# A transformer block in float32: compression inputs and keys split at full width and copied between partitions by DMA, memory's sums of squares on ScalarE, softmax weights of two heads at a time

## The chip, the cores and the metric

One core of a Trainium2 chip runs the program. The metric is the time of one execution on the device in microseconds (us). The kernel before takes 458.88 us, the median of three runs (458.44 to 459.89).

The engines are TensorE (PE in the rows, its weight loads PEld), VectorE (DVE), ScalarE (ACT), GpSimd (POOL) and SyncE (SP). Each takes its instructions strictly in the order in which they stand in its queue, and each waits by semaphore for what an instruction needs. DMAs are issued from the queues of SyncE, ScalarE and GpSimd.

## The reference

One layer at width 1024 over 256 tokens: a sparse attention mixer ("NSA"), then cross attention to 256 memory tokens, then a gated feed-forward block with a three-tap convolution, with RMS norms between them and after the last. Only the first part and memory's norm are touched by the change:

```
h = rmsnorm(x)
q, kc, vc, ks, vs, kw, vw, gl = split(h @ w_in)          # q: 16 heads of 64; the others: 4 groups of 64
k_cmp = gelu(blocks(kc) @ ck_w1) @ ck_w2                 # blocks of 32 tokens, stride 16: 15 per group
v_cmp = gelu(blocks(vc) @ cv_w1) @ cv_w2
p_cmp = softmax(q . k_cmp);  p_sel = softmax(q . ks);  p_win = softmax(q . kw)     # per head, causal
o = g0 * p_cmp @ v_cmp + g1 * p_sel @ vs + g2 * p_win @ vw                         # g = sigmoid(gl)
x = x + o @ w_out
mem_n = rmsnorm(mem)
```

With 256 tokens all four selection blocks are always chosen and the window covers everything, so the selected and the window branch are both plain causal attention, each with its own keys and values.

## The kernel before, in words

**Float32 by halves.** Every product in full precision is made from rounded operands and their remainders: an operand `x` becomes `hi`, which ScalarE writes as a rounded copy, and `lo = x - hi`, which VectorE computes. `mm3` then issues three matmuls (hi.hi, lo.hi, hi.lo), on lines 187 to 189.

**Weights.** 512 KB half chunks (128 x 1024) come from HBM in one fixed order. `half` (line 127) loads each into `raw`, splits it with one ScalarE copy (line 120) and one VectorE subtraction (line 124), up to `AHEAD = 4` half chunks before TensorE uses it. There are `NBUF = 6` buffers of `hi` and of `lo`: half chunk number n takes the buffer of number n - 6 and so waits until TensorE has finished with that one. Numbered by chunk and half, the rows below have hi5 = keys of the selected branch (`w_ks`), hi6 and hi7 = the first weights of key compression (`w_ck`), hi8 and hi9 = of value compression (`w_cv`), hi10 = window keys (`w_kw`). So hi8_1 takes the buffer of hi5_1.

**Order of the work.** The queues of SyncE and GpSimd are filled in the order of the code. TensorE, VectorE and ScalarE are ordered at build time by a scheduler that runs a timeline of its own; the order is then fixed. In the first stage `between(first(), ...)` emits, a step at a time, the projections (`compress_in(0)`, `queries(0)`, `compress_in(1)`, `keys(0)`), then `hidden(0)` and `hidden(1)`, then `keys(1)` and `queries(1)`, and starts side jobs (`rms`, `gated`) at given steps; `later` hands it a job that runs on beside the stream.

**Compression inputs.** `compress_in(j)` (j = 0 for keys, 1 for values) makes `pc` in PSUM: 64 channels of two groups on partitions 0 to 63 and 64 to 127, tokens along the free axis. Line 462 multiplies it in place by the tokens' norm factor `row`. The hidden product needs another layout, `B[0]` (in the rows c200 for j = 0 and c210 for j = 1): even tokens on partitions 0 to 63, odd ones on 64 to 127. Four ScalarE copies of 64 partitions (two of them read one half of the partitions and write the other) make the hi part, four VectorE subtractions the lo part, all straight from PSUM. GpSimd copies the shifted second half of each block into `B[1]` (c201, c211; line 480) and puts the positional term `pe` into a spare column of `B[0]` (line 482).

**Hidden product.** `hidden(j)` takes `B` as the stationary operand, 32 matmuls into `pM` (line 531), two for every k tile. It uses eight half chunks in all for j = 0 and 1. A ScalarE copy `hsb` and two transposes into `pH` follow, then a short chain of GELU.

**Keys.** `keys(br)` multiplies `pk` by `row` into a spare tile, then ScalarE rounds it into `KH` and copies the other half of the partitions too (four copies of 64 partitions), and VectorE makes `KL` (two subtractions, line 509).

**Gates.** `gated` makes a small product `pg`, transposes it (`pgt`, just before the last four matmuls of `pk`), adds its two parts on VectorE, takes two tanh on ScalarE (line 597) and writes `gates` on VectorE (line 600).

**Attention.** 32 heads-and-tiles (`Head`) run as a software pipeline: scores, mask and row minimum on VectorE (line 826), exponent on ScalarE (line 832), then on VectorE a reciprocal, a product with the gate and two multiplications, one a branch (lines 837 to 840), then transposes on TensorE (line 846), a copy on ScalarE (line 850) and the value product (line 868). Between them `advance` hands TensorE a share of the projections for memory (`fill`) as filler.

**Memory's norm.** `mem_rms` takes half of each row's sum of squares on ScalarE and half on VectorE.

## Time and profile before

| | us |
|---|---|
| median of three runs | 458.88 |
| the profiled execution | 459.02 |
| its span in the trace | 457.1 |
| TensorE busy, of the span | 445.2 (97%) |
| VectorE, ScalarE, GpSimd busy | 324.2, 288.9, 42.7 |
| share of the chain that ended last on TensorE | 85% |

The profiled execution took 1.9 us more than its span, which is what lies around the span. The rows name lines of the kernel before, tiles without their buffer numbers, and say in brackets what ended an engine's wait. A TensorE row's duration includes the way through the array, so back to back matmuls overlap; how close they follow shows in their starts.

### The profile page before, as it was taken

The page shows a single profiled execution, that of the slowest core. Times are in us where ns is not written, and L with a number is a line of the kernel's source. Part 1 is how long each engine was busy: PE and PEld are TensorE (multiplying, and loading weights), DVE is VectorE, ACT ScalarE, POOL GpSimd, SP SyncE. Part 2 cuts the span into 40 slices and gives each one's busy share as a digit, 9 for nine tenths or more (in the row PEclk, how much of TensorE's full clock was granted, in tenths as well). Part 3 has the DMA queues.
Part 4 walks back from the last instruction along what each step waited for, and adds up shares of the span by engine and source line. Part 5 has one row for each costly group of instructions (what it writes and reads, how often), then busy time and mean ns, then how long its engine had stood idle before and what let it go on. Part 6 is the DMA issues. An engine that isn't in the chain of part 4 may idle for free.

```text
span 457.1 us, 8682 instructions
## 1 busy us (share of the span) xinstructions
PE 445.2 (97%) x3276; PEld 412.1 (90%) x3276; DVE 324.2 (71%) x694; ACT 288.9 (63%) x591; POOL 42.7 (9%) x82
## 2 busy tenths in 40 slices
PE   8999799999999999999999999999999999999994
PEld 5999799999998778999998899999999999888984
DVE  4788989798888895846643857878777777745413
ACT  6796689677887886865553757666666666535301
POOL 4332001221200000200000010000000000001003
PEclk9999899999999999999999999999999999999998
DMA  8997775543422005555334437755555555564302
GB/s 293 363 412 261 242 241 167 181 122 111 139 94 92 3 1 181 162 156 187 102 104 170 150 128 210 246 186 184 187 180 185 184 189 179 189 188 151 128 0 93
DMA packets 22077, 77.05 MB, mean 169 GB/s; under 512 B 2579, under 2 KB 3091, under 8 KB 22035
## 3 DMA queue, kind: packets, MB, share of 16 engines
q1 hardware_dynamic: 21312, 74.39, 48.7%
q10 hardware_dynamic: 720, 2.10, 1.4%
q8 instruction: 26, 0.43, 0.4%
q14 instruction: 19, 0.13, 0.1%
HBM read 75.43 MB, written 1.05 MB: 167 GB/s over the span
## 4 chain that ended last, share of the span: by engine, by line
PE 85%; DVE 6%; DMA 4%; ACT 2%; issue 2%; SPq 0%; POOLq 0%; DVEq 0%; ACTq 0%; POOL 0%
PE up L187 8%; PE up L189 8%; PE up L188 8%; PE pd L189 5%; PE pd L187 4%; PE pd L188 4%; PE O L868 2%; DVE lo L124 2%; PE pt L846 2%; DMA raw<-in_w_ks 2%; PE pcq L187 2%; PE pmk L189 2%; PE pmk L188 2%; PE pmk L187 2%; PE pmv L189 2%
## 5 line engine op out<-in xcount | busy, mean ns | idle before, releaser
L124 DVE TENSOR_TENSOR lo<-raw,hi 128x1024 fp32r<-128x1024 f32 x130 | 158.6, 1227 | 60.2 <-ACT hi L120 59.3
L120 ACT ACTIVATE hi<-raw 128x1024 fp32r<-128x1024 f32 x130 | 136.8, 1058 | 55.1 <-PE pd L189 17.7
L187 PE MATMUL up<-h_hi,hi 128*128 128x256 f32 x304 | 86.3, 284 | 0.0
L189 PE MATMUL up<-h_hi,lo 128*128 128x256 f32 x304 | 86.2, 284 | 0.0
L188 PE MATMUL up<-h_lo,hi 128*128 128x256 f32 x304 | 86.2, 284 | 0.0
L188 PEld LDWEIGHTS up<-h_lo,hi 128*128 128x128 f32 x304 | 58.4, 192 | 0.0
L189 PEld LDWEIGHTS up<-h_hi,lo 128*128 128x128 f32 x304 | 58.4, 192 | 0.0
L187 PEld LDWEIGHTS up<-h_hi,hi 128*128 128x128 f32 x304 | 58.4, 192 | 0.0
L189 PE MATMUL pd<-hi,aT_lo 128*128 128x512 f32 (+1 forms) x110 | 38.5, 350 | 0.0
L188 PE MATMUL pd<-lo,aT_hi 128*128 128x512 f32 (+1 forms) x110 | 38.5, 350 | 0.0
L187 PE MATMUL pd<-hi,aT_hi 128*128 128x512 f32 (+1 forms) x110 | 38.4, 349 | 0.0
L832 ACT ACTIVATE pp<-pp,nm 128x128 f32<-128x128 f32 (+1 forms) x64 | 28.4, 447 | 5.8 <-DVE nm L826 5.6
L826 DVE CUSTOM_DVE_ANT_0 pp<-s,tri,nrs 128x128 f32<-128x128 f32 (+1 forms) x64 | 24.1, 412 | 2.4 <-PE pt L846 2.0
L188 PEld LDWEIGHTS pd<-lo,aT_hi 128*128 128x128 f32 x110 | 20.7, 188 | 2.9
L189 PEld LDWEIGHTS pd<-hi,aT_lo 128*128 128x128 f32 x110 | 20.7, 188 | 2.9
L187 PEld LDWEIGHTS pd<-hi,aT_hi 128*128 128x128 f32 x110 | 20.7, 189 | 2.9
L1110 ACT ACTIVATE th<-c 128x256 f32<-128x256 f32 x22 | 9.1, 414 | 22.2 <-DVE c L1108 22.2
L850 ACT ACTIVATE pT<-pt 128x256 f32<-128x256 f32 (+1 forms) x32 | 15.3, 482 | 9.2 <-PE pt L846 8.9
L840 DVE TENSOR_SCALAR pp<-pp,den 128x128 f32<-128x128 f32 (+1 forms) x64 | 19.8, 349 | 0.6
L189 PE MATMUL pmv<-hi,memT_lo 128*128 128x256 f32 x64 | 18.6, 290 | 0.0
L188 PE MATMUL pmv<-lo,memT_hi 128*128 128x256 f32 x64 | 18.5, 289 | 0.0
L189 PE MATMUL pq<-hT_hi,lo 128*128 128x256 f32 x64 | 18.5, 289 | 0.0
(309 smaller groups left out, 1149.2 us busy)
## 6 DMA issues: line engine op xcount, KB each, us to landing
raw<-in_w_up SPq DMA_DIRECT2D x44, 512.0 KB, 4.6
raw<-in_w_dn SPq DMA_DIRECT2D x20, 512.0 KB, 3.8
raw<-in_w_q SPq DMA_DIRECT2D x8, 512.0 KB, 5.1
raw<-in_w_mk SPq DMA_DIRECT2D x8, 512.0 KB, 5.0
raw<-in_w_mv SPq DMA_DIRECT2D x8, 512.0 KB, 3.7
raw<-in_w_out SPq DMA_DIRECT2D x8, 512.0 KB, 3.8
raw<-in_ca_wq SPq DMA_DIRECT2D x8, 512.0 KB, 4.7
raw<-in_ca_wo SPq DMA_DIRECT2D x8, 512.0 KB, 4.2
```

The lines of the kernel that those rows point to most:

```text
L120: nc.scalar.activation(his[i][h], raws[i][h], AF.Copy)
L124: nc.vector.tensor_tensor(t, raws[i][h], f(his[i][h]), op=ALU.subtract)
L187: nc.tensor.matmul(ps, lh, rh, start=start, stop=False)
L188: nc.tensor.matmul(ps, lh, rl, start=False, stop=False)
L189: nc.tensor.matmul(ps, ll, rh, start=False, stop=stop)
L826: nc.vector.tensor_tensor_reduce(self.ppv[:, br], sv[:, br], tri[:, 1 - t:], nrs[:, t:t + 1], 3e38, ALU.add, ALU.min, self.nm[:, br:br + 1])
L832: nc.scalar.activation(self.ppv[:, br], self.ppv[:, br], AF.Exp, bias=self.nm[:, br:br + 1], scale=-1.0, accum_out=self.den[:, br:br + 1])
L840: nc.vector.tensor_scalar(self.ppv[:, br], self.ppv[:, br], den[:, br:br + 1], None, op0=ALU.mult)
L846: nc.tensor.transpose(self.pt[:, o:o + P], self.pp[:, o:o + P], ident)
L850: nc.scalar.activation(self.pT[:, :self.w], self.pt[:, :self.w], AF.Copy)
L868: nc.tensor.matmul(O[r:r + DK, m * P:(m + 1) * P], V[:, blk // 2, blk % 2, g, :], group[i].pT[:, blk * P:(blk + 1) * P], start=False, stop ...
L1110: nc.scalar.activation(th, c, AF.Tanh, scale=0.5)
```

## The change

Five things, in the words of the code. `CW = 6` is new.

1. `compress_in`: line 462's product goes to a spare piece of SBUF (`v`, in `xT`) with even and odd tokens apart, instead of back to PSUM. Four DMAs of 64 partitions, issued from GpSimd's queue, carry it into the layout of `B` (`vp`). After six steps one ScalarE copy and one VectorE subtraction at 128 partitions split it. GpSimd's copies become one for `B[1]` and one for `pe`. Columns are numbered by group, not by block (`NC` 60 becomes 64), and what reads them follows.
2. `keys`: the product is split at 128 partitions into a tile `T`, and six DMAs from GpSimd's queue carry T into `KH` (both halves of the partitions) and `KL`. `KH` and `KL` now hold the branches one after the other (`br`, then tile).
3. `mem_rms`: both sums of squares on ScalarE.
4. Heads in pairs: `weigh` once for two heads, with one product of two tensors in place of four multiplications by a column; `transposed` and `copied` in units of one full PSUM bank.
5. The pipeline's driver calls the pair's steps on every second turn.

```diff
@@ compress_in
-                B = [cp.tile([P, 8, 2, 64], F32R, name=f"c2{j}{i}") for i in range(2)]
+                B = [cp.tile([P, 8, 2, 2, 2, 16], F32R, name=f"c2{j}{i}") for i in range(2)]
+                rows = [z.rearrange("p jj x g m n -> p (jj x g m) n") for z in B]
...
                 def out(ps):
                     yield from wait("row")
-                    nc.vector.tensor_tensor(both, both, row.unsqueeze(1).to_broadcast([P, 2, S]), op=ALU.mult)
-                    split((B[1][:, :, 0, NC], B[1][:, :, 1, NC], cc[:, o + 8:o + 16]),
-                          (pe[:, 0, :, 0], pe[:, 1, :, 0], cc[:, o:o + 8]))
...
-                    for hi, lo, v_ in items:
-                        split_hi(hi, v_)
-                    yield
-                    for hi, lo, v_ in items:
-                        split_lo(lo, hi, v_)
-                    for x in range(2):
-                        nc.gpsimd.tensor_copy(B[1][:, :, x, 0:NC], f(B[0][:, :, x, G:16 * G]))
-                    for x in range(2):
-                        nc.gpsimd.tensor_copy(B[0][:, :, x, NC:NC + 1], f(pe[:, x]))
+                    v, vp = (xT[:, k:k + 2].rearrange("p k s -> p (k s)") for k in ((6, 2), (4, 6))[j])
...
+                    nc.vector.tensor_tensor(v.rearrange("p r m c -> p m c r"),
+                                            ps.rearrange("p (m c r) -> p m c r", m=2, r=2),
+                                            row.rearrange("p (c r) -> p c r", r=2).unsqueeze(1).to_broadcast(
+                                                [P, 2, 128, 2]), op=ALU.mult)
                     for gp in range(2):
                         for par in range(2):
...
+                            nc.gpsimd.dma_start(vp[par * 64:par * 64 + 64, gp].rearrange("p c jj -> p (c jj)"),
+                                              v[gp * 64:gp * 64 + 64, par].rearrange("p m c -> p (m c)"))
+                    split((B[1][:, :, 0, 0, 0, PEC], B[1][:, :, 1, 0, 0, PEC], cc[:, o + 8:o + 16]),
+                          (pe[:, 0, :, 0], pe[:, 1, :, 0], cc[:, o:o + 8]))
+                    yield from pause(CW)
+                    hi, lo = (B[0][:, :, x].rearrange("p jj g m n -> p g (m n) jj") for x in range(2))
+                    split_hi(hi, vp)
+                    yield
+                    split_lo(lo, hi, vp)
+                    nc.gpsimd.tensor_copy(rows[1][:, :, 0:PEC], f(rows[0][:, :, 1:16]))
+                    nc.gpsimd.tensor_copy(B[0][:, :, :, 0, 0, PEC].rearrange("p jj x -> p x jj"), f(pe[:, :, :, 0]))
                     done.add(f"c2{j}")
@@ keys
+                    T = xT[:, 4:8].rearrange("p (x m) s -> p x m s", x=2).bitcast(F32R)
+                    split_hi(T[:, 0], v)
+                    yield
+                    split_lo(T[:, 1], T[:, 0], v)
                     for gp in range(2):
...
-                        split_hi(hi, v_)
-                        items.append((hi, lo, copy, v_))
-                    yield
-                    for hi, lo, _, v_ in items:
-                        KE.tensor_tensor(lo, v_, f(hi), op=ALU.subtract)
-                    for _, _, hi, v_ in items:
-                        split_hi(hi, v_)
+                        for x, z, r in ((0, KH, own), (0, KH, oth), (1, KL, own)):
+                            nc.gpsimd.dma_start(
+                                f(z[r].rearrange("p (m gp) b h k -> p m gp b (h k)", gp=2)[:, :, gp, br]),
+                                f(T[own, x]))
@@ mem_rms
-                    sums = [sumsq(mem[:, :512], f"mem{t}a"), sumsq(mem[:, 512:], f"mem{t}b", dve=True)]
+                    sums = [sumsq(mem[:, :512], f"mem{t}a"), sumsq(mem[:, 512:], f"mem{t}b")]
@@ Head, Pair
                 def weigh(self):
-                    den = self.den
+                    den, w = self.den, (1 + self.t) * P
                     nc.vector.reciprocal(den, den)
-                    nc.vector.tensor_tensor(den, den, gates[:, self.g, self.t, self.i, 1:3], op=ALU.mult)
-                    for br in range(2):
-                        nc.vector.tensor_scalar(self.ppv[:, br], self.ppv[:, br], den[:, br:br + 1], None,
-                                                op0=ALU.mult)
+                    nc.vector.tensor_tensor(den, den, gates[:, self.g, self.t, 2 * self.m:2 * self.m + 2, 1:3], op=ALU.mult)
+                    pv_ = self.pp.rearrange("p j b k -> p (j b) k")[:, :, :w]
+                    nc.vector.tensor_tensor(pv_, pv_, den.rearrange("p j b -> p (j b)").unsqueeze(2).to_broadcast(
+                        [P, 4, w]), op=ALU.mult)
...
+                    def pair(f, lag):
+                        if (n - lag) % 2 and 0 < n - lag < len(heads):
+                            f(pairs[(n - lag) // 2])
```

**How the queues change.** ScalarE's queue before, from the split of the selected keys' first weights on; c200 is `B[0]` of the keys, c210 of the values.

```order
L120 ACTIVATE hi5_0_363<-raw5_0_361 128x1024 [waits DMAHW3_49,DVE_49]
L192 ACTIVATE c200_256<-pc0_260 64x2x16x8 [waits DVE_49]
L120 ACTIVATE hi5_1_381<-raw5_1_379 128x1024 [waits DMAHW4_49]
...
L192 ACTIVATE c210_449<-pc1_453 64x2x16x8 [waits DVE_49]
L120 ACTIVATE hi7_0_523<-raw7_0_521 128x1024
L585 ACTIVATE gsb_583<-pg_559 96x256 [waits PE_49]
...
L120 ACTIVATE hi8_0_635<-raw8_0_633 128x1024 [waits DMAHW6_49,PE_49]
L120 ACTIVATE hi8_1_652<-raw8_1_650 128x1024 [waits DMAHW7_49,PE_49]
```

The same queue after the change, at the place where c200 and c210 stand now.

```order
L121 ACTIVATE hi8_0_627<-raw8_0_625 128x1024 [waits DMAHW6_49,DVE_49,PE_49]
L597 ACTIVATE gt_597<-gt_597,hrs_248 128x48 [waits DVE_49,Pool_49]
...
L121 ACTIVATE hi8_1_643<-raw8_1_641 128x1024 [waits DMAHW7_49,PE_49]
L193 ACTIVATE c200_256<-xT_100 128x64x8 [waits DMASW2_49,DMASW3_49,DMASW1_49,DMASW0_49]
L217 ACTIVATE sq_mem1a_1118,ss_mem1a_1117<-mem1_1049 128x512 [waits DMAHW2_49]
...
L193 ACTIVATE c211_446<-cc_71 128x8 [waits Pool_49]
...
L121 ACTIVATE hi9_1_678<-raw9_1_676 128x1024 [waits DMAHW1_49,PE_49]
L193 ACTIVATE c210_445<-xT_100 128x64x8 [waits DMASW6_49,DMASW7_49,DMASW5_49,DMASW4_49]
L193 ACTIVATE xT_100<-xT_100 128x512 [waits DVE_49]
L121 ACTIVATE hi10_0_693<-raw10_0_691 128x1024 [waits DMAHW3_49,PE_49,Activation_49]
L121 ACTIVATE hi10_1_709<-raw10_1_707 128x1024 [waits DMAHW4_49,PE_49,Activation_49]
L538 ACTIVATE hsb0_701<-pM0_624 128x256 [waits PE_49]
```

The split of c200 stood ahead of hi5_1 and stands behind hi8_1 now; that of c210 stood ahead of hi7_0 and stands behind hi9_1, ahead of the copy `hsb0` of the first hidden product.

GpSimd's queue before, from the norm factor's diagonal on.

```order
L247 TENSOR_SCALAR dg_x_391<-ident_74,rs_x_101 128x128 [waits Pool_49]
L480 CAST c201_257<-c200_256 128x8x60 [waits Activation_49]
L480 CAST c201_257<-c200_256 128x8x60 [waits DVE_49]
L482 CAST c200_256<-pe0_258 128x8 [waits Pool_49] x2
L443 TENSOR_SCALAR nrs_247<-rs_x_101 128x2
L444 TENSOR_SCALAR hrs_248<-rs_x_101 128x2
L456 MEMSET c211_450 128x16x3
```

The same stretch after the change, up to the first DMA of the values.

```order
L248 TENSOR_SCALAR dg_x_391<-ident_74,rs_x_101 128x128 [waits Pool_49]
L474 DMA xT_100<-xT_100 64x256 [waits DMAHW5_49,DMAHW2_49,DVE_49]
L474 DMA xT_100<-xT_100 64x256 x3
L443 TENSOR_SCALAR nrs_247<-rs_x_101 128x2
L444 TENSOR_SCALAR hrs_248<-rs_x_101 128x2
L483 CAST c201_257<-c200_256 128x64x15 [waits DVE_49]
L484 CAST c200_256<-pe0_258 128x2x8 [waits Pool_49]
L460 MEMSET c211_446 128x64
L474 DMA xT_100<-xT_100 64x256 [waits DMASW0_49]
```

The four DMAs for the values stand behind the two copies of the keys' blocks, which wait for VectorE's part of c200.

VectorE's queue after the change, at c200.

```order
L593 COPY gt_597<-pgt_591 128x96 [waits PE_49]
L594 TENSOR_TENSOR gt_597<-pgt_591,gt_597 128x96 [waits DVE_49]
L125 TENSOR_TENSOR lo8_0_631<-raw8_0_625,hi8_0_627 128x1024 [waits DMAHW6_49,Activation_49]
...
L125 TENSOR_TENSOR lo8_1_647<-raw8_1_641,hi8_1_643 128x1024 [waits DMAHW7_49,PE_49,Activation_49]
L197 TENSOR_TENSOR c200_256<-xT_100,c200_256 128x64x8 [waits DMASW2_49,DMASW1_49,DMASW3_49,DMASW0_49,Activation_49]
L497 TENSOR_TENSOR xT_100<-pk0_516,xT_100 128x512 [waits DVE_49]
```

The subtraction for c200, which stood third behind the product by `row` before, stands behind lo8_1 now. On TensorE the first matmul of the hidden product follows the last of `pk` directly, before and after, and waits for ScalarE's, VectorE's and GpSimd's parts of c200; after the change all 32 matmuls of the second hidden product stand behind the two transposes `pH` of the first.

## Rows read from the trace of the kernel before

**Rows 1.** The page's engine shares and the granted clock in 40 slices.
```profile
PE 445.2 (97%) x3276; PEld 412.1 (90%) x3276; DVE 324.2 (71%) x694; ACT 288.9 (63%) x591; POOL 42.7 (9%) x82
PEclk9999899999999999999999999999999999999998
```

**Rows 2.** Busy time by stretches: us, engines' busy us (instructions), clock, DMA, GB/s.
```profile
40.00:50.00 10.00, 8.47 (x66) 7.72 (x65) 8.76 (x12) 7.89 (x13) 3.69 (x4) 1.00 0.67 214
50.00:60.00 10.00, 8.44 (x54) 7.79 (x53) 8.68 (x17) 8.29 (x15) 0.00 (x0) 0.83 0.78 252
60.00:70.00 10.00, 10.00 (x86) 10.00 (x85) 9.73 (x18) 8.54 (x13) 0.00 (x0) 1.00 0.68 221
...
160.00:170.00 10.00, 9.38 (x75) 7.40 (x74) 9.70 (x47) 9.25 (x32) 0.27 (x1) 1.00 0.01 2
```

**Rows 3.** The same view in short stretches of the hidden products.
```profile
48.00:49.00 1.00, 0.18 (x1) 0.00 (x0) 1.00 (x2) 0.97 (x2) 0.00 (x0) 1.00 0.88 324
...
54.00:57.00 3.00, 3.00 (x16) 3.00 (x15) 3.00 (x5) 1.70 (x2) 0.00 (x0) 0.50 0.75 220
```

**Rows 4.** TensorE in order of time: start, us, operation, wait before it.
```profile
42.65 0.38 PE L589 MATMUL pgt<-ident,gsb 96*128 96x96 f32 x2 [0.39 <-ACT gsb L585]
...
43.25 0.28 PE L189 MATMUL pk<-hT_hi,lo 128*128 128x256 f32 x1
43.82 0.36 PE L531 MATMUL pM<-hi,c 128*128 128x256 f32 x1 [0.29 <-DVE c L196]
...
49.03 0.38 PE L531 MATMUL pM<-lo,c 128*128 128x256 f32 x1 [0.85 <-DVE lo L124]
...
52.30 0.44 PE L542 MATMUL pH<-ident,hsb 128*128 128x128 f32 x2
53.53 0.39 PE L531 MATMUL pM<-lo,c 128*128 128x256 f32 x1 [0.80 <-DVE lo L124]
...
63.15 0.28 PE L189 MATMUL pq<-hT_hi,lo 128*128 128x256 f32 x1
```

**Rows 5.** ScalarE in order of time, 27 to 53 us.
```profile
27.52 2.59 ACT L192 ACTIVATE c<-pc 64x256 fp32r<-64x256 f32 x4
...
39.17 0.33 ACTq L894 DMA_DIRECT2D mem<-in_mem  x1
...
43.75 1.99 ACT L120 ACTIVATE hi<-raw 128x1024 fp32r<-128x1024 f32 x2
...
49.68 0.56 ACT L597 ACTIVATE gt<-gt,hrs 128x48 f32<-128x48 f32 x2
50.26 0.63 ACT L192 ACTIVATE KH<-xT 64x512 fp32r<-64x512 f32 x1
```

**Rows 6.** VectorE in order of time, 27 to 53 us.
```profile
30.14 2.56 DVE L196 TENSOR_TENSOR c<-pc,c 64x256 fp32r<-64x256 f32 x4 [1.27 <-ACT c L192]
...
46.83 0.26 DVE L593 COPY gt<-pgt 128x96 f32<-128x96 f32 x1
...
52.26 1.22 DVE L124 TENSOR_TENSOR lo<-raw,hi 128x1024 fp32r<-128x1024 f32 x1
```

**Rows 7.** GpSimd in order of time, 16 to 46 us.
```profile
30.17 0.59 POOL L480 CAST c<-c 128x480 fp32r<-128x480 f32 x1 [5.74 <-ACT c L192]
32.76 1.65 POOL L480 CAST c<-c 128x480 fp32r<-128x480 f32 x1 [2.00 <-DVE c L196]
34.35 0.33 POOL L482 CAST c<-pe 128x8 fp32r<-128x8 f32 x2
```

**Rows 8.** DMA issues: queue, count, KB each, median us from issue to landing.
```profile
mem<-in_mem ACTq DMA_DIRECT2D x2, 512.0 KB, 6.7
...
out<-y SPq DMA_DIRECT2D x1, 256.0 KB, 2.0
```

**Rows 9.** Groups of instructions: busy us, mean ns of one, idle before them.
```profile
L840 DVE TENSOR_SCALAR pp<-pp,den 128x128 f32<-128x128 f32 (+1 forms) x64 | 19.8, 349 | 0.6
...
L837 DVE RECIPROCAL den<-den 128x2 f32<-128x2 f32 x32 | 5.1, 158 | 4.2 <-ACT pp L832 4.0
```

More of the change, by code (lines that the diff above doesn't have):

```diff
@@ L425, in trunk_kernel @@
             row = xT[:, 0]
-            free = [xT[:, k:k + 2] for k in (2, 4)]
             nrs = at.tile([P, NT], F32, name="nrs")
@@ L814, in scores @@
                     self.s = bank("S", f"s{self.name}")[:, :self.w]
-                    nc.tensor.matmul(self.s, q, khv, start=True, stop=False)
-                    nc.tensor.matmul(self.s, q, klv, start=False, stop=True)
+                    nc.tensor.matmul(self.s, q, KH[:, g, :, :n], start=True, stop=False)
+                    nc.tensor.matmul(self.s, q, KL[:, g, :, :n], start=False, stop=True)
                 def biggest(self):
-                    t = self.t
-                    self.pp = aq.tile([P, 512], F32, tag="pp", name=f"pp{self.name}", bufs=3)
@@ L821, in biggest @@
[L821 to L823 removed]
+                    pair, t, j = self.pair, self.t, self.i % 2
+                    if j == 0:
+                        pair.pp = aq.tile([P, 2, 2, 256], F32, tag="pp", name=f"pp{self.name}", bufs=2)
+                        pair.nm = small.tile([P, 2, 2], F32, tag="nm", name=f"nm{self.name}")
+                        pair.den = small.tile([P, 2, 2], F32, tag="den", name=f"den{self.name}")
@@ L872, in summed @@
-                def summed(self):
-                    g, tq = self.g, slice(self.t * P, (self.t + 1) * P)
-                    if self.i == HPG - 1:
-                        split((oT[0][:, 2 * g:2 * g + 2, tq], oT[1][:, 2 * g:2 * g + 2, tq],
-                               Os[g, self.t][:, :256].rearrange("p (c s) -> p c s", c=2)))
+                    blocks = [(j, br, h) for j in range(2) for br in range(2) for h in range(1 + self.t)]
+                    self.at = {b: divmod(n, 4) for n, b in enumerate(blocks)}
@@ new lines, in transposed @@
+                    self.pt = [bank("PT", f"pt{self.g}{self.t}{self.m}{n}") for n in range(len(blocks) // 4)]
+                    for (j, br, h), (n, o) in self.at.items():
+                        nc.tensor.transpose(self.pt[n][:, o * P:(o + 1) * P], self.pp[:, j, br, h * P:(h + 1) * P], ident)
+                def copied(self):
+                    self.pT = []
+                    for n, pt in enumerate(self.pt):
+                        self.pT.append(aq.tile([P, 4, P], F32, tag="pT", name=f"pT{self.g}{self.t}{self.m}{n}", bufs=5))
+                        nc.scalar.activation(self.pT[n].rearrange("p o k -> p (o k)"), pt, AF.Copy)
@@ new lines, in block, with values @@
+                def block(self, j, br, h):
+                    n, o = self.at[j, br, h]
+                    return self.pT[n][:, o]
+            def values(pairs_):
+                g, t = pairs_[0].g, pairs_[0].t
+                O = Os[g, t] = bank("O", f"O{g}{t}")
+                for m in range(2):
+                    nc.tensor.matmul(O[:, m * P:(m + 1) * P], Vc[:, g, m, :], pcT[:, g, t, :],
+                                     start=m == 0, stop=False, skip_group_check=True)
+                blocks = [(br, h) for br in range(2) for h in range(1 + t)]
+                for pair in pairs_[::-1]:
+                    for br, h in blocks:
+                        for j in (1, 0):
+                            nc.tensor.matmul(O[j * DK:(j + 1) * DK, pair.m * P:(pair.m + 1) * P], V[:, h, br, g, :],
+                                             pair.block(j, br, h), start=False, stop=(br, h) == blocks[-1],
+                                             skip_group_check=True)
@@ L928, in trunk_kernel @@
             UNITS = [(0, 0), (0, 1), (1, 0), (1, 1), (2, 0), (3, 0), (2, 1), (3, 1)]
-            heads = [Head(g, t, i) for g, t in UNITS for i in range(HPG)]
-            for n, h in enumerate(heads):
-                h.n = n
+            pairs = [Pair(g, t, m) for g, t in UNITS for m in range(2)]
+            heads = [h for pair in pairs for h in pair.heads]
             with tc.manual_schedule(engines=M2):
```

131 lines of the change are left out of this document (56 added, 75 removed).

## The prediction

> **What bounds the kernel now.** I read the page first: TensorE is busy for 97% of the span and its clock is full but for two slices [rows 1]. Busy time by tens of microseconds then tells where it is not: 1.5 us of 40 to 50 and 1.6 us of 50 to 60 are idle, the second of these at a mean clock of 0.83, while 60 to 70 is full with 86 matmuls, 0.116 us each; in 160 to 170 it lacks 0.6 us, with VectorE and ScalarE at 9.7 and 9.3 [rows 2]. So nearly everything is TensorE's own work, which the change leaves as it is (the same matmuls in another order). What it can win or lose lies in those two places.
>
> The first is the two hidden products. TensorE in order of time shows `pM` held up by weights that VectorE or ScalarE has not split: 0.85 us at 49.03 and 0.80 at 53.53, and only 0.29 us at its start, 43.82 [rows 4]. In short stretches TensorE does next to nothing in 48 to 49, and 54 to 57 runs at 0.50, the lower level of 1.2 GHz, with 16 matmuls in 3 us where the full level fits 26 [rows 3]. From `pM`'s start to the end of `pk` (63.15) 19.3 us pass; 64 matmuls of `pM`, 48 of `pk` and the small ones are 13.6 us at 0.116. So 5.7 us are lost there.
>
> **The change, part by part.** *Work taken off.* Eight copies of `c` at 0.65 us on ScalarE become two, eight subtractions at 0.64 on VectorE two [rows 5, 6]; the keys' copies of 0.63 go from eight to two; a sum of squares per memory tile moves to ScalarE. VectorE loses about 6 us of 27 to 60, ScalarE about as much. By busy time alone the 5.7 us would be there to win. But the engines take their queues in order, and the order has changed.
>
> *c200, first half.* ScalarE's part of c200 now stands behind hi8_1, and hi8_1 takes the buffer of hi5_1, which `pk` reads to its last matmul. I follow that. In the trace that matmul starts at 43.25; the transposes `pgt` ahead of it had waited 0.39 us for a ScalarE that was busy with c210, and that goes, so it starts at 42.85 and is through at 43.1, `pgt` at 42.6 [rows 4]. Ahead of hi8_1 stand the two tanh, which need `pgt`, then two small operations on VectorE, 0.26 us each [rows 6]: VectorE done at 43.2, tanh (0.56) at 43.8, hi8_1 (half of 1.99) at 44.8 [rows 5]. Then c200 on ScalarE to 45.7, while VectorE does lo8_1 (1.22) to 46.1 and then its part of c200 to 47.0 [rows 6].
>
> The price of these two full-width splits isn't in the trace. A copy of 512 elements in runs costs 0.63, one of 256 in the scattered layout 0.65 [rows 5]; so 0.63 if the scatter comes free now that the source is SBUF, 1.3 if it costs per element as before. VectorE's rows say 0.64 to 1.28 in the same way [rows 6]. I take 0.85 for each, nearer to the run of 512 since source and sink are both SBUF there.
>
> A rule bears on that choice. The Trainium skill (SBUF — State Buffer, section Door 1, on cachelines) says that an access which crosses to another 16-byte line pays, so that float32 may be strided only a little for free; each element of the new split is still written 512 bytes from the one before. By the rule it is 1.3 and the end comes 1 us later than in my sum; by the row of runs it is 0.63 and 0.5 us sooner.
>
> *c200, second half.* GpSimd must now wait for VectorE's part, copy 960 elements (two copies of 480 at 0.59 with no VectorE beside, so 1.2) and write `pe` (0.2 of 0.33) [rows 7]. Before, the first product's own copies were done at 34.7, nine microseconds early. Now they end at 48.4, and the first matmul of `pM` starts at 48.5 instead of 43.82: TensorE stands still for 5.4 us from 43.1 on.
>
> *c210.* The four DMAs for the values stand on GpSimd's queue behind those copies, so they cannot go out before 48.5 either, though their data has been ready since about 38. What one issue costs on GpSimd no row shows. ScalarE's queue issues one in 0.33 [rows 5]; a GpSimd instruction takes 0.2 to 1.65 [rows 7]. I take 0.7, twice ScalarE's, and keep 0.33 and 1.65 for the range: issued at 51.4. Landing took 2.0 us where the DMA engines were quiet and 6.7 where they were full [rows 8]; by then TensorE has stood still and loads wait for buffers, so 2.0: landed at 53.4. ScalarE, in order: c210 0.85, T 0.63, hi10_0 and hi10_1 2.0, and only then `hsb`, some 0.4; `pH` 0.44 [rows 4, 5]. So `pH` is through at 57.8. VectorE's and GpSimd's way to c210 (0.85 and 1.4 behind 54.3, and perhaps the waits of rival B) ends at about the same time. The first `pM` ends at 52.2 and the second starts at 57.8: another 5.6 us of standing still.
>
> *The sum in this place.* Second `pM` 3.7 us to 61.5, `pk` 5.6, transposes and the small key product 0.6: 67.7, against 63.3 for the same work before. That is 4.4 us lost, at full clock. The 5.7 us lost before include a stretch of 3 us at 0.50 that followed about 2.5 us of idling in 48 to 54 [rows 3]; with holes twice as long I expect the lower level again, and count the same 1.7 us where matmuls run: 6.1 us. If the level falls in the holes and is back when work is, it costs nothing; if it falls twice where matmuls run, 3.4.
>
> *c0's DMAs, the keys' DMAs, memory's sums.* The keys' four DMAs go out at 27, into full DMA engines; even at 6.7 us and more they have landed by 37, eight microseconds before ScalarE asks. The twelve DMAs into `KH` and `KL` are needed at the first scores, at 88 and later now; nothing on the way is late unless an issue costs over 1.5 us. Memory's squares lie in ScalarE's wait for c210. I count these at nothing; what hides them is the hole.
>
> *Heads in pairs.* The multiplications by a column, 19.8 us in 64, become 8 products of 512 elements (0.7, as a split of 512 costs) and 8 of 1024 (1.22), 15.4 us; reciprocals and gate products, 5.1 us and as much again, are halved [rows 6, 9]. VectorE has 9.5 us less over 85 to 170. TensorE is full for most of that with filler, so it counts only where filler has run out, in 150 to 170: 0.6 us are idle in 160 to 170, and the slice ahead of it is much the same, so some 1.3 [rows 2]. The order of pairs makes the steps coarser. I take 0.9 gained, of 0 to 1.3.
>
> Sum against the profiled execution: 459.0 + 6.1 - 0.9 = 464.2; its time is 0.1 above the median, so 464.
>
> **The rivals.** *A: the hole closes (faster).* If c200 and c210 were split long before `pk` ends, the work taken off would count in full: `pM` would start at 43.2 and run with `pk` to 57.1, 6 us sooner, and with the pairs the time would be 452. For it: VectorE full in 40 to 60 and the waits for lo [rows 2, 4]. Against it: the queue orders, in which only a wait for `pk`'s last buffer stands ahead of c200. It decides from the point where hi8_1 doesn't wait for hi5_1's last reader, or where the built order isn't the one that runs. 8%.
>
> *B: GpSimd's issues are dear.* A copy by GpSimd that takes 0.59 alone took 1.65 beside a VectorE split, 32.76 to 34.41, the length of that split and its own [rows 7]. If each of c210's four issues waits like that, they cost 1.65 each, 3.8 us more, and with some more for the keys' twelve the time is 468 to 469. Against it: few VectorE operations run in the hole. 22%.
>
> The Trainium skill (SBUF — State Buffer, section Who interferes with whom) says that GpSimd writes a DMA's descriptors through a port pair that VectorE's two-port operations lock, and that a two-tensor operation takes only the reading half of it; by that rule the splits don't hold the issues up, and B loses. No run here shows it yet.
>
> *C: the second hole is short.* With 0.33 an issue, 0.63 a split and no lower clock, the second `pM` starts at 55.5 and the end comes 2.1 later than before, less 1.3 from the pairs: 459.8, hardly to be told from no change. For it: the cheap ends are all from rows. Against: all three must come together. 10%.
>
> **How the numbers follow.** The forecast has 60%, with a range of its own of 461.5 to 467 (0.33 to 1 us an issue, clock loss 0 to 3.4). A measurement here tells 0.3%, 1.4 us, from no change. B lies above, C at the lower edge. A range of 460 to 469 leaves out A, the lower part of C and the worst of B, with everything dear (471). Faster by more than 0.3% is A: 0.08. Within it is most of C and a little of the forecast: 0.10. Slower: 0.82.
>
> **What would show it.** In the profile after: the first `pM` waits some 5 us with GpSimd's `pe` copy as its releaser, starting at 47.5 to 49.5; hi8_1 starts behind the tanh at about 43.8, c200 right behind it though its DMAs landed before 40; c210 waits on ScalarE for a DMA issued behind the copies; `pH` follows at 55 to 60; the granted clock falls in 45 to 65. In 150 to 170 TensorE's waits shrink by about a microsecond. I am wrong if c200 is split before 43, if TensorE starts `pM` before 46, or if the second hole is under 2 us; and wrong in size if an issue on GpSimd takes over 1 us or the level stays full.

## The result and the profile after

The kernel after took 466.7 us (median of 4 runs, 466.1 to 467.3) where the kernel before, on the same chip, took 459.0: a ratio of 1.016 (95% interval 1.0145 to 1.0179), 7.7 us slower. The prediction was 464.0 in a range of 460 to 469. The profiled spans are 457.1 and 465.0 us. Two profiled executions of the runs below, e1's (2464 us) and e9's (499 us), ran slow from end to end and are left out of the times.

The engine shares and the granted clock, after, against [rows 1]:

```profile
PE 445.1 (96%) x3276; PEld 413.3 (89%) x3276; DVE 314.6 (68%) x602; ACT 282.0 (61%) x575; POOL 49.6 (11%) x99
PEclk9999799989999999999999999999999999999998
```

VectorE has 9.6 us less to do, ScalarE 6.9, GpSimd 6.9 more; TensorE has the same. Less work made a longer kernel.

TensorE in order of time, after (start, us, operation, wait before it and its releaser), against [rows 4]:

```profile
42.72 0.28 PE L190 MATMUL pk<-hT_hi,lo 128*128 128x256 f32 x1
...
48.28 0.58 PE L531 MATMUL pM<-hi,c 128*128 128x256 f32 x1 [5.28 <-POOL c L484]
...
56.60 0.44 PE L542 MATMUL pH<-ident,hsb 128*128 128x128 f32 x2 [2.77 <-ACT hsb L538]
56.86 0.38 PE L531 MATMUL pM<-hi,c 128*128 128x256 f32 x1
...
91.05 0.46 PE L756 MATMUL psc<-ident,sT 64*128 64x64 f32 x4 [1.26 <-ACT sT L745]
```

The holes that the prediction named are there: 5.28 us ahead of the first `pM`, released by GpSimd's copy of `pe`, and 2.77 ahead of `pH`, behind which the second `pM` stands. A third place, at 91 us, is new. ScalarE in order of time, after:

```profile
43.65 1.04 ACT L121 ACTIVATE hi<-raw 128x1024 fp32r<-128x1024 f32 x1
44.60 1.09 ACT L193 ACTIVATE c<-xT 128x512 fp32r<-128x512 f32 x1
...
51.86 1.06 ACT L121 ACTIVATE hi<-raw 128x1024 fp32r<-128x1024 f32 x1 [0.63 <-PE pM L531]
52.83 1.14 ACT L193 ACTIVATE c<-xT 128x512 fp32r<-128x512 f32 x1
53.76 0.64 ACT L193 ACTIVATE xT<-xT 128x512 fp32r<-128x512 f32 x1
54.29 1.99 ACT L121 ACTIVATE hi<-raw 128x1024 fp32r<-128x1024 f32 x2
56.18 0.37 ACT L538 ACTIVATE hsb<-pM 128x256 f32<-128x256 f32 x1
...
85.04 3.31 ACT L193 ACTIVATE memT_hi<-MV,cc 128x256 fp32r<-128x256 f32 x8 [3.32 <-DMA KL<-xT]
```

Three queue orders are read here. c200 starts straight behind hi8_1, though its DMAs went out at 28; c210 straight behind hi9_1, with no wait for a DMA; and `hsb`, a copy of 0.37 us for which TensorE stands still, comes 3.4 us behind c210's start, behind three splits. GpSimd in order of time, after, against [rows 7]:

```profile
28.04 2.32 POOL L474 DMA_DIRECT2D xT<-xT  x4 [3.54 <-DVE xT L468]
...
46.97 0.98 POOL L483 CAST c<-c 128x960 fp32r<-128x960 f32 x1 [16.17 <-DVE c L197]
48.01 0.21 POOL L484 CAST c<-pe 128x16 fp32r<-128x16 f32 x1
...
48.25 2.10 POOL L474 DMA_DIRECT2D xT<-xT  x4
...
56.26 0.55 POOL L484 CAST c<-pe 128x16 fp32r<-128x16 f32 x1
```

GpSimd stood 16 us behind a wait with c210's four DMAs queued after it. The last row is its part of c210, which ends at 56.81: the second `pM`, at 56.86, could not have begun sooner had `hsb` come earlier. Short stretches, after (us; busy us and instructions of TensorE, its weight loads, VectorE, ScalarE, GpSimd; clock; DMA share; GB/s), against [rows 2, 3]:

```profile
48.00:51.00 3.00, 2.72 (x12) 2.72 (x13) 0.17 (x1) 1.04 (x2) 2.34 (x6) 0.50 0.77 244
...
57.00:60.00 3.00, 3.00 (x27) 3.00 (x27) 2.79 (x5) 0.10 (x1) 3.00 (x6) 1.00 0.69 197
...
92.00:96.00 4.00, 3.88 (x19) 3.82 (x20) 3.93 (x10) 3.11 (x8) 0.00 (x0) 0.58 0.74 224
```

Behind the first hole TensorE ran 12 matmuls in 3 us at the lower level, where 27 fit at the full one; behind the second the level stayed full; behind the third it fell again (0.58).

To see where time is lost and not won back, I added up the matmul columns of TensorE's timeline in each kernel (both have the same) and read how much later the other kernel reaches the same sum, at marks of the kernel before. "After" is 4.5 us behind at 60, 4.9 at 84.5, 8.0 at 96, and 7.5 at 441. The marks are good to some half a microsecond, since a column costs more in a short matmul (60 columns took 0.11 us, 256 took 0.12) and the two kernels have theirs in another order. So in this profile the loss has two parts: 4.9 in the hidden products, 3.1 near 91. The runs below that take one part away put the sizes otherwise: 6.9 for the compression inputs alone, 1.5 for the stall near 91.

The third place, in the chain of waits of after (start, us, what):

```profile
76.33 8.39 DMA KL<-xT
...
85.85 2.50 ACT memT_hi L193 x6
...
90.59 0.68 DVE QS L617
```

`T`, the source of the window keys' DMAs, lies in `xT`, and the memory's split `memT_hi` is written to the same place. It may not be written until the last DMA has read `T`; that one went out at 76.33 and was 8.39 us under way. In the kernel before this split starts at 72.00 with no wait.

### The profile page after: what moved, and what is told of

It reads as the page before. It is cut to its first block, busy times and chain, and to the rows that moved or that the text cites. A ratio compares the mean times of both kernels' runs of the same rounds, so it can differ in the third digit from the quotient of the medians.

```text
span 465.0 us, 8593 instructions
## 1 busy us (share of the span) xinstructions
PE 445.1 (96%) x3276; PEld 413.3 (89%) x3276; DVE 314.6 (68%) x602; ACT 282.0 (61%) x575; POOL 49.6 (11%) x99
## 4 chain that ended last, share of the span: by engine, by line
PE 86%; ACT 4%; DMA 3%; DVE 3%; issue 2%; POOL 1%; SPq 0%; POOLq 0%; DVEq 0%; ACTq 0%
PE up L190 8%; PE up L189 8%; PE up L188 8%; PE pd L188 4%; PE pd L189 4%; PE pd L190 4%; PE O L883 2%; PE pt L859 2%; PE pv L403 2%; DMA KL<-xT 2%; PE pmk L188 2%; PE pmk L189 2%; PE pmk L190 2%; PE pcq L188 2%; PE pcq L189 2%
## 5 line engine op out<-in xcount | busy, mean ns | idle before, releaser
L1164 POOL TENSOR_TENSOR xw<-x_sb,wfin 128x512 f32<-128x512 f32 (+1 forms) x2 | 3.9, 1952 | 155.7 <-DVE x_sb L1147 155.7
L189 PE MATMUL pmk<-memT_lo,hi 128*128 128x256 f32 x64 | 19.0, 297 | 0.0
L188 PE MATMUL pmk<-memT_hi,hi 128*128 128x256 f32 x64 | 18.8, 294 | 0.2 <-DVE QS L617 0.2
L190 PE MATMUL pmk<-memT_hi,lo 128*128 128x256 f32 x64 | 18.8, 294 | 0.0
```

Of the source, the lines that this page charges most:

```text
L188: nc.tensor.matmul(ps, lh, rh, start=start, stop=False)
L189: nc.tensor.matmul(ps, lh, rl, start=False, stop=False)
L190: nc.tensor.matmul(ps, ll, rh, start=False, stop=stop)
L1164: nc.gpsimd.tensor_tensor(xw[:, cs], x_sb[:, 1, cs], wfin[:, cs], op=ALU.mult)
```

## The experiments

The theory: the loss comes from where instructions stand in three queues, and from whose buffer `T` is; not from their durations, nor from the pairs of heads. The rivals: that the new operations (full-width splits, GpSimd's copies and issues) are dear by themselves, and that another part of the change carries part of the loss. Ratios are to the kernel before, with 95% intervals. Places are better evidence than the end of a single profile, since some profiles lose 1.0 to 1.6 us at 25 us (last section).

**The parts of the change.** e2 is the kernel before with the heads in pairs (and their layout of `KH` and `KL`) alone. Its edit is the diff's part at Head and Pair.

> The kernel before with the heads in pairs alone (and the new order of branches inside KH and KL that the pairs read). Theory M: the pairs are worth the 0.5 us by which the distance between the two kernels shrinks from 100 to 170 us: 458.5, no stall at 85 to 95. Rival R2 (the coarser steps cost the stall at 89 us): 461 to 462. A third reading, that the pairs' 9.5 us of VectorE are worth more where nothing else is late: 457 or less.

Measured: 459.05, ratio 0.9992 (0.998 to 1.0004). The pairs win nothing that ten runs can tell. e9 is the kernel before with the new compression inputs alone:

```
+  nc.gpsimd.dma_start(vp[...], v[...])     # four for each hidden product
   ...
+  yield from pause(CW)
   ...
+  split_hi(hi, vp); yield; split_lo(lo, hi, vp)
+  nc.gpsimd.tensor_copy(rows[1][:, :, 0:PEC], f(rows[0][:, :, 1:16]))
```

> The kernel before with the new compression inputs alone; keys, memory's sums and heads as before. Theory M (the holes in the hidden products are the inputs' work, the stall at 89 us that of the keys' DMAs): the first pM at 48 us, the second at 56 to 57, some 5 us lost there, and no stall at 89, since memory's split waits for no DMA: 464 to 464.5. Rival (the inputs carry the whole 7.7, and the keys' DMAs nothing, as the difference to the kernel with the old inputs says): 466 to 467. Rival (the parts need each other): under 461.

Measured: 466.1 (465.25 to 466.62, four runs), ratio 1.0151 (1.0126 to 1.0176). The inputs alone cost 6.9 us of the 7.7, and `memT_hi` waits for no DMA there. TensorE in order of time shows the same hole and releaser:

```profile
55.22 0.58 PE L534 MATMUL pM<-hi,c 128*128 128x256 f32 x1 [5.23 <-POOL c L485]
```

e3 is the reverse, the kernel after with the inputs as before:

```
-  split_hi(hi, vp); yield; split_lo(lo, hi, vp)
   ...
+  for hi, lo, v_ in items: split_hi(hi, v_)     # four of 64x256
+  yield
+  for hi, lo, v_ in items: split_lo(lo, hi, v_)
```

> The kernel after with the compression inputs as before (four copies and four subtractions out of PSUM, no DMA); keys by DMA, memory's sums and pairs stay. Theory M: the hidden products start at 43 to 44 us again and the 5.2 us lost there come back; the wait of memT for KL's DMAs stays: 461 to 462. Rival R1 (DMAs from GpSimd's queue as such are the cost, those of the keys as much as those of the inputs): 463.5 to 465, with the twelve that are left still disturbing. Rival R3 (the keys' or the sums' part opens the holes in the hidden products): no better than 466.

Measured: 459.24, ratio 1.0008 (0.9996 to 1.0021). All the rest of the change together costs nothing. By the columns it is 1.7 us ahead of the kernel before at 60 us, and 1.1 behind at 96: what is left of the change, the keys at full width among it, gains in the hidden products and gives it back later, where `memT_hi` starts at 81.31 instead of 72.00, though it waits for no DMA there; e7 below asks whether that is the cause.

**The third place.** e1 gives `T` of the second keys the buffer of c200, which is free by then:

```
+  if br:
+      T = cp.tile([P, 2, 2, S], F32R, tag="c200", name="T1")
```

> Edit: the second branch's split T goes to the buffer of c200, which is no longer read, instead of xT, whose place memory's split memT takes next. The DMAs into KH and KL stay. Theory M (the loss at 89 us is ScalarE's memT split waiting until the last DMA of KL has read T): ScalarE writes memT at about 73 instead of 85, TensorE's idling at 89 to 91 and the half clock behind it go, 3.1 us less: 463.6. Rival R1 (the DMAs into KH and KL are late in themselves, and the first scores wait for them): 466 to 467, with the wait moved from memT to the scores. Rival R2 (the pairs make the start of attention late): no change, 466.7.

Measured: 465.15 (464.4 to 465.7, three runs), ratio 1.0125 (1.0108 to 1.0142). About 1.5 us less than after; the expectation was 3.1. e11 is the same kernel once more, for its profile.

> The same kernel as in e1, for a profile: there the profiled execution ran at a sixth of TensorE's speed and shows nothing, while the timed ones gave 465.4 against 466.7 of the kernel after. Theory M: the wait of memory's split at 85 us is gone, and of the 3.1 us lost between 85 and 98 in the kernel after 1.3 are won; the rest is still lost at another place between 60 and 100. Rival: the wait stays, now for a later user of that place.

Measured: 465.59. `memT_hi` of e11, by tile (lines, first and last start), has lost its wait, and so has the clock's fall in 92 to 96:

```profile
L193 ACT ACTIVATE memT_hi<-MV,cc x8: 491/492/510, 73.7 to 77.4; 128x256 fp32r<-128x256 f32 x8
```
```profile
92.00:96.00 4.00, 4.00 (x31) 3.57 (x31) 3.89 (x11) 1.78 (x6) 0.00 (x0) 1.00 0.71 253
```

By the columns it goes from 6.0 behind at 84.5 to 6.3 at 96, where after goes from 4.9 to 8.0, so the stall's cause is shown. But this execution was 1.3 us late at 37 already; why the timed runs won 1.5 and not 3 the runs don't settle. e7 has the inputs as before and e1's buffer.

> The kernel with the old compression inputs (e3, 459.2), and besides the second branch's T in c200's buffer, so that memory's split doesn't wait for the DMAs that read T. In e3 this stretch (60 to 75 us) lost 2.8 us against the kernel before, and ahead of it the keys split at full width had won 1.5. Theory M: the loss goes, the gain stays: 456.5 to 457.5, faster than both kernels. Rival (the DMAs into KH and KL themselves, or the readers of KH, hold the attention up): 458.5 to 459.5. Rival (a later user of c200's place waits for them instead): 458 to 459, with the wait at the first heads' weights.

Measured: 458.9 (10 runs), ratio 1.0005 (0.9991 to 1.0018). `memT_hi` starts at 66.24 instead of 81.31, and that wins nothing that 10 runs can tell: its profiled execution, 1.2 us ahead by the columns at 441, is also the fastest of the ten. So the late `memT_hi` is not shown to be what e3 gives back; that stays open.

**The hidden products.** e4 moves c200's splits ahead of hi7_0 and lo7_0, and c210's ahead of hi9_0 and lo9_0:

```
+  early, AFTER = {}, {(7, 0): 0, (9, 0): 1}
   ...
+  with behind("hi", i, h):          # issued after the split of c2j0
       nc.scalar.activation(his[i][h], raws[i][h], AF.Copy)
   ...
+  with behind("lo", i, h):
       nc.vector.tensor_tensor(t, raws[i][h], f(his[i][h]), op=ALU.subtract)
```

> The kernel after, with issue order alone changed: on ScalarE and VectorE the split of c200 stands ahead of hi7_0 and lo7_0 and of the gates' copy, that of c210 ahead of hi9_0 and lo9_0, and the product for the keys behind lo8_0. Same instructions, same DMAs. Theory M (the place of c200's split behind pk's last buffer is the cause): first pM at 43 to 43.5 us instead of 48.3, the second, bound by the DMAs of c210 issued behind GpSimd's copies at 39 to 41, at about 50.5 instead of 57; the loss at 89 us stays: 460 to 462. Rival R1 (DMA traffic and the late loads of the weights are the cause, not the order): pM starts early but stalls for weights, 465 or more.

Measured: 469.12 (466.04 to 471.49), ratio 1.0223 (1.0163 to 1.0283). The first hole went, but the wait ahead of the second `pM` grew to 6.45 us. TensorE, GpSimd and ScalarE of e4, in order of time:

```profile
54.06 0.58 PE L540 MATMUL pM<-hi,c 128*128 128x256 f32 x1 [6.45 <-POOL c L492]
...
66.50 0.44 PE L551 MATMUL pH<-ident,hsb 128*128 128x128 f32 x2 [2.75 <-ACT hsb L547]
```
```profile
40.20 1.93 POOL L491 CAST c<-c 128x960 fp32r<-128x960 f32 x1 [8.77 <-DVE c L205]
...
43.29 2.11 POOL L482 DMA_DIRECT2D xT<-xT  x4
```
```profile
50.17 1.07 ACT L201 ACTIVATE c<-xT 128x512 fp32r<-128x512 f32 x1 [3.33 <-DMA xT<-xT]
...
65.12 1.06 ACT L126 ACTIVATE hi<-raw 128x1024 fp32r<-128x1024 f32 x1 [3.37 <-DMA raw<-in_w_q]
```

GpSimd's copies were twice as long beside VectorE's splits, c210's DMAs went out behind them at 43.29, and ScalarE waited for their landing. Here the step "c210 waits on ScalarE for a DMA issued behind the copies", which after itself does not show, decides over the second hole. It does not explain the time: by the columns (table below) e4 loses 1.7 us from 37 to 60, where after loses 4.4, and then 4.7 from 60 to 84.5, where after loses next to nothing. There the second `pH` waits 2.75 us for a `hsb` that stands on ScalarE behind a weight split, which waits 3.37 us for its load, and the clock behind it is 0.59 (68 to 72). e6 is after with those four DMAs ahead of GpSimd's copies, and nothing else; e5 is e4 with it:

```
+  done.add(f"in{j}")           # the DMAs of hidden product j are out
   ...
+  if j == 0:
+      yield from wait("in1")
   nc.gpsimd.tensor_copy(rows[1][:, :, 0:PEC], f(rows[0][:, :, 1:16]))
```

> The kernel after with the values' four DMAs ahead of GpSimd's copies and nothing else. Theory M: the first product isn't touched (c200's split is still behind hi8_1): 48.3 us. In the kernel after ScalarE came to c210 at 52.8 and didn't wait for its DMA, so the second hole is set by the queues of ScalarE and VectorE: no more than 1 us is won, 465.5 to 467. Rival (the prediction's step: the second hole is the DMAs issued behind the copies): second pM 2 to 3 us earlier, 463.5 to 464.5.

Measured: 468.32, ratio 1.0211 (1.0193 to 1.0228), 1.6 us more than after. TensorE of e6:

```profile
49.39 0.58 PE L534 MATMUL pM<-hi,c 128*128 128x256 f32 x1 [5.22 <-POOL c L487]
...
75.46 0.40 PE L663 MATMUL pvc<-w2v,gv 128*15 128x64 f32 x4 [0.80 <-POOL gv L656]
```

ScalarE's order keeps the first hole; ahead of `pH` 1.55 us are left of 2.77. What is won there goes again behind it: 3.6 us from 60 to 84.5, where the products `pvc` of the compressed values wait twice, 0.80 and 0.77, for GpSimd's `gv` (2.44 us for two, 0.69 in after), and the clock is 0.73 in 76 to 80.

> As the kernel with the splits of c200 and c210 early (e4), and besides the four DMAs of the values stand on GpSimd's queue ahead of its two copies of the keys' blocks, not behind them; in e4 they went out at 43.3 us though their data had been ready since 37.3, and ScalarE then waited 3.3 us for them until 50.2. Theory M2 (the second product waits for DMAs that stand behind GpSimd's copies): issued at 37.3 to 39.5, landed by 46 at a landing of 6 us, c210 split on ScalarE by 48, on VectorE and GpSimd by 49.5; the second pM starts at about 49.5 instead of 54.1: some 4.5 us less than e4 in the hidden products, of which up to 2 come back as a longer wait of memT at 85: 465 to 466 against 469. Rival (the loads of the weights hold the DMAs up, whenever they are issued): they land at 50 again, 468 to 469. Rival (GpSimd's copies, slow beside VectorE, are the price): the second pM still at 53 or later.

Measured: 463.16, ratio 1.0108 (1.0085 to 1.013). Each half alone made the time no shorter, both together win 3.5 us. From 37 to 60 e5 loses 1.8 us, as much as e4; what sets it apart is that the later waits of e4 and e6 don't come (0.2 lost from 60 to 84.5), and why they don't is not shown. The second `pM` still waits. TensorE, GpSimd and ScalarE of e5:

```profile
52.69 0.58 PE L543 MATMUL pM<-hi,c 128*128 128x256 f32 x1 [5.41 <-POOL c L495]
```
```profile
36.62 2.11 POOL L482 DMA_DIRECT2D xT<-xT  x4 [5.29 <-DVE xT L476]
...
49.92 1.57 POOL L494 CAST c<-c 128x960 fp32r<-128x960 f32 x1 [6.73 <-DVE c L205]
51.55 1.08 POOL L495 CAST c<-pe 128x16 fp32r<-128x16 f32 x1
```
```profile
46.48 0.63 ACT L225 ACTIVATE sq_mem1a<-mem 128x512 bf16<-128x512 f32 x1 [2.35 <-DMA mem<-in_mem]
47.72 1.05 ACT L201 ACTIVATE c<-xT 128x512 fp32r<-128x512 f32 x1
```

Now memory's squares wait for their load ahead of c210 (`sq_mem1a`, which was ScalarE's before too; the change put a second one behind it), and the copies end 4.9 us after c210's split began. e8 adds e1's buffer to e5.

> The kernel after with all three: the splits of c200 and c210 early, the values' DMAs ahead of GpSimd's copies, the second branch's T in c200's buffer. Theory M2: as e5 with memT's wait gone: 1.5 to 3 us below e5, 462 to 464. Still above the kernel before, since c210 still passes product, DMA, two splits and GpSimd's copy one after the other before its first matmul. Rival (the holes are all of the loss): 459 or below.

Measured: 462.77, ratio 1.0089 (1.007 to 1.0108); the second `pM` waits 4.82 us. e10 fills the holes with work: e6, with the second keys' products and weights ahead of both hidden products:

```
   yield from keys(0)
+  yield from keys(1)
   yield from hidden(0, compressed_keys)
   yield from hidden(1, compressed_values)
-  yield from keys(1)
```

> The kernel after with the values' DMAs ahead of GpSimd's copies (e6), and the second branch's keys moved ahead of the hidden products, in the loads of the weights and in the code. TensorE then has the 48 matmuls of pk (5.6 us) between the first branch's keys and the first hidden product, and the queries between the two products. Theory M (what costs is that TensorE has nothing else to do while c200 and c210 pass through DMA, two splits and GpSimd; the work of the splits themselves is less than before): both holes close to under 1.5 us together, memory's split no longer waits for KL's DMAs, which go out some 15 us earlier: 455 to 458. Rival (the late loads of the weights or the half clock cost the time, whatever order TensorE has): 462 or more. Rival (the order moves the wait to the values' chain, which now ends last ahead of the attention): 459 to 461.

Measured: 469.52 (467.44 to 470.92), ratio 1.0228 (1.0189 to 1.0267). Both holes shrank, to 0.92 and 1.20 us (2.0 us ahead at 60), and the waits came up later. TensorE and ScalarE of e10:

```profile
60.57 0.39 PE L190 MATMUL pq<-hT_hi,lo 128*128 128x256 f32 x1 [1.81 <-DVE lo L125]
...
88.57 0.39 PE L188 MATMUL pmk<-memT_hi,hi 128*128 128x256 f32 x1 [3.14 <-ACT memT_hi L193]
```
```profile
88.01 3.30 ACT L193 ACTIVATE memT_hi<-MV,cc 128x256 fp32r<-128x256 f32 x8 [3.98 <-DMA KL<-xT]
```

Queries wait for a `lo` that VectorE has not split yet, and the clock falls behind that wait (0.57 in 62 to 66, 23 matmuls in 4 us). Then the second keys' `T`, written in place of the first's, sends its DMAs late, and `memT_hi` waits for them. It is 10.4 behind at 96, so 12 us are given back. e12 is e8 with the second keys between the two hidden products.

> The kernel with all three (e8: splits early, the values' DMAs ahead of GpSimd's copies, the second branch's T in c200's buffer), and the second branch's keys between the two hidden products, in the weights' order and in the code: the 48 matmuls of pk (5.6 us) stand where TensorE stood still. In e10, with the keys ahead of both products, the stretch to 60 us was 3.4 us shorter than before the keys' DMAs came into play, but T was overwritten in place and memory's split waited for KL's DMAs until 88 us. Here that wait is gone by T's place. Theory M2: first pM at 43.3 to 44, pk behind it, second pM at 52.8 to 53.5, no hole over 1 us; 2 to 3.5 us less than the kernel before: 455.5 to 457.5. Rival (the weights' splits are late for the stream without holes, as for the queries in e10, 1.8 us): 457.5 to 459. Rival (the values' chain now ends last ahead of the attention, with all that hangs on it): 460 or more.

Measured: 463.37 (460.83 to 463.56), ratio 1.0086 (1.0066 to 1.0105). The second hole is 1.46 us, and a wait of 3.19 at 73 takes its place. TensorE, GpSimd, VectorE and ScalarE of e12:

```profile
56.82 0.38 PE L546 MATMUL pM<-hi,c 128*128 128x256 f32 x1 [1.46 <-POOL c L496]
...
73.02 0.42 PE L196 MATMUL pkc<-gh,w2h 128*128 128x64 f32 x1 [3.19 <-ACT gh L201]
```
```profile
49.28 6.13 POOL L495 CAST c<-c 128x960 fp32r<-128x960 f32 x1 [6.38 <-DVE c L205]
```
```profile
49.92 4.63 DVE L131 TENSOR_TENSOR lo<-raw,hi 128x1024 fp32r<-128x1024 f32 x4
```
```profile
69.47 3.30 ACT L201 ACTIVATE memT_hi<-MV,cc 128x256 fp32r<-128x256 f32 x8 [4.74 <-DMA KL<-xT]
```

GpSimd's copy, 0.98 us in after, takes 6.13 beside a run of VectorE's splits; `memT_hi` waits for a DMA again, one of the first branch, whose T still lies in `xT`; that one went out at 59.61, behind GpSimd's copies, and `gh` stands behind `memT_hi` on ScalarE.

No version beats the kernel before; e2, e3 and e7 equal it. Of the 7.7 us, order and buffer together give back 3.9, by the medians (e8). There the second `pM` still waits 4.82 us, for a c210 that passes ScalarE's split (from 47.99), VectorE's and GpSimd's copies (to 52.90) one after the other. So order is shown as the cause of the first hole, and the buffer as the cause of `memT_hi`'s wait; whether that path would cost the rest in every order is not shown, and so the rival that the new operations are dear by themselves stands for this rest. The distance to the kernel before by equal matmul columns, in us (its own times at the head):

| | 37 | 60 | 84.5 | 96 | 167 | 441 |
|---|---|---|---|---|---|---|
| after | 0.1 | 4.5 | 4.9 | 8.0 | 7.5 | 7.5 |
| e3 | 0.5 | -1.7 | 0.0 | 1.1 | 0.7 | 0.7 |
| e4 | 1.0 | 2.7 | 7.4 | 8.3 | 7.7 | 7.8 |
| e5 | 0.1 | 1.9 | 2.1 | 4.2 | 3.7 | 3.7 |
| e6 | 1.2 | 4.0 | 7.6 | 8.9 | 8.4 | 8.4 |
| e7 | -0.1 | -2.2 | -1.3 | -1.3 | -1.0 | -1.2 |
| e8 | 1.5 | 2.1 | 2.1 | 3.2 | 3.8 | 4.3 |
| e10 | 1.4 | -2.0 | 4.7 | 10.4 | 11.3 | 11.4 |
| e11 | 1.3 | 5.8 | 6.0 | 6.3 | 6.3 | 6.3 |
| e12 | 1.6 | -2.0 | 1.9 | 3.8 | 4.0 | 4.0 |

## Why the prediction was right, point by point

*The first hole: right.* Predicted start of `pM` 48.5, of hi8_1 43.8, with c200 right behind; measured 48.28, 43.65 and 44.60. The releaser is the one named. e4 shows that the place in the queue is the cause: with c200 moved forward the first `pM` starts at 43.72, with no wait. The terms: a split 1.09 and 1.03 us, taken as 0.85; GpSimd's copy 0.98, taken as 1.2; `pe` 0.21 as 0.2.

The Trainium skill (SBUF — State Buffer, section Door 1, on cachelines) was weighed there against the row of runs, 1.3 against 0.63. The split of `T`, which runs through its rows, took 0.64, and the scattered one of as many elements 1.14 in the same stretch: the rule's direction holds, at about three quarters of the extra cost that the prediction set against it.

*The second hole: right in its end, wrong in its middle.* `pH` was predicted through at 57.8 and starts at 56.60. The step that failed is "they cannot go out before 48.5 ... landed at 53.4" as what holds ScalarE up: four issues took 2.10, 0.52 each, where 0.7 was taken, the last landed at 52.57, and ScalarE reached c210 at 52.83 with no wait for a DMA left, behind a hi9_1 that had waited 0.63 for `pM` and that the prediction left out of ScalarE's order. `hsb` stood behind c210, `T`, hi10_0 and hi10_1 all the same, and VectorE's and GpSimd's way to c210 ended with it, as predicted (56.81). The DMAs' lateness was a second bound just under the first, as e4 and e6 show: with either alone the other holds. The hole itself was 2.77 us, half of the 5.6 predicted, since the first `pM` ran on to 53.8 at the lower clock, which the prediction counted apart.

*The clock: right in size.* In this stretch the lower level came once where matmuls run: sixteen of `pM` took from 48.28 to 51.78, 3.5 us, and take 1.9 at the full level, 0.118 apart, so 1.6 were lost where 1.7 were counted. (The 1.7 fits the mean clock of 0.83 in 50 to 60 [rows 2]; the row that is cited, 16 matmuls where 26 fit in 3 us [rows 3], says 1.2.) The stretch as a whole lost 4.9 by the columns, predicted 6.1; the inputs alone cost 6.9 (e9).

*Rival B.* Its condition was issues of 1.65 us; the longest took 0.77. The Trainium skill (SBUF — State Buffer, section Who interferes with whom) speaks for that: a two-tensor operation of VectorE takes only the reading half of the shared ports, and a DMA's descriptors need the writing half. The trace agrees: four issues took 2.32 us beside two splits of VectorE at 28, and 2.10 while VectorE was nearly idle.

```profile
28.05 2.33 DVE L125 TENSOR_TENSOR lo<-raw,hi 128x1024 fp32r<-128x1024 f32 x2
```

*The pairs: wrong in size.* 0.9 us were counted, e2 shows 0. The operations came out as estimated, by the groups of after:

```profile
L850 DVE TENSOR_TENSOR pp<-pp,den 128x1024 f32<-128x1024 f32 x8 | 9.8, 1223 | 0.2
L850 DVE TENSOR_TENSOR pp<-pp,den 128x512 f32<-128x512 f32 x8 | 5.5, 688 | 0.1
```

VectorE's relief is real and off the path. In 150 to 170 e2 lacks 1.2 us of TensorE, 0.2 and 1.0 in its two halves, where the kernel before lacks 0.6 in each: the wait moved and did not shrink. The second half, with VectorE and ScalarE at 9.2 and 8.5:

```profile
160.00:170.00 10.00, 8.96 (x54) 6.82 (x50) 9.22 (x31) 8.54 (x32) 0.22 (x1) 1.00 0.01 2
```

*The keys' DMAs: the term that was mis-sized.* "I count these at nothing; what hides them is the hole" asked when their destination is needed (the first scores) and not when their source is overwritten. `memT_hi` waited 3.32 us, and by the columns 3.1 were lost; without the wait the runs took 1.5 less (e1), so its size is not settled. By the columns the whole is 4.9 plus 3.1, less 0.5 won back behind 96: 7.5; the forecast had 6.1 - 0.9. The errors were 1.2 too much in the hidden products, 0.9 for the pairs that did not come, and 3.1 for a stall that was not seen. That the range held the time is in part luck: it was not made for this stall, and the hidden products' excess offset a part of it.

*Rivals A and C* did not come. The instructions ran in the order built, so A's condition failed. Of C's three only the full clock held, and only behind the second hole; a split took 1.09 and 1.14, an issue 0.52.

## What to carry to other kernels

A rewrite that takes work off two engines can lose more than it saves by where its instructions now stand: look for a short copy behind a split that waits (e4's `hsb`, 2.75 us), for a short split behind full-width ones (c200, 5.28 us), and for DMA issues behind a wait on GpSimd's queue. For each DMA that is added, ask twice: when is its destination read, and when is its source written again. Where two queues each hold a product back, moving one alone may show nothing in the time, as in e4 and e6: read by place what it won there and where that went again, and try the two together before either is dismissed.

## What the runs showed of the hardware

- *GpSimd beside VectorE.* The same copy of 960 elements took 0.98 us in after, 1.93 beside two splits (e4), 1.57 beside others in e5, and 6.13 beside a run of four (e12). The Trainium skill (SBUF — State Buffer, section Who interferes with whom) says that a VectorE instruction with two inputs in SBUF contends with a GpSimd instruction that reads there; the runs agree, and in e12 GpSimd's copy ended only when the run of splits had (55.41 and 54.55).
- *Small DMAs between partitions.* Issues of 64 and 128 KB from GpSimd took a median of 5.1 to 6.2 us to land beside the weights' loads, 8.4 for the one that `memT_hi` waited for:

```profile
KH<-xT POOLq DMA_DIRECT2D x8, 128.0 KB, 6.1
...
xT<-xT POOLq DMA_DIRECT2D x8, 64.0 KB, 5.1
...
KL<-xT POOLq DMA_DIRECT2D x4, 128.0 KB, 6.2
```

- *Profiles differ early.* At 25 us GpSimd's two `dg_x` run beside VectorE; in e11 they took 3.22 us and TensorE waited 0.77 for them, in after they took 2.12:

```profile
22.55 3.22 POOL L248 TENSOR_SCALAR dg_x<-ident,rs_x 128x128 f32<-128x128 f32 x2
```

In the profiled executions of e4, e6, e8, e10, e11 and e12 `dg_x` took 3.2 us, and they were 1.0 to 1.6 us late at 37 by the columns. In those of before, after, e5 and e7 it took 2.1 to 2.2, and they were not late; e3, with 2.0, was 0.5 late. Each of these kernels has one such profile, so whether the kernel or the execution decides is not shown. So the ends of two single profiles can't be compared to better than that.
